# FFN input weights: the low half of each second 1024 columns comes from an accumulating DMA instead of a VectorE subtraction

## The chip, the core and the metric

The kernel runs on one core of a Trainium2 chip. The metric is the device time of one execution in microseconds (us). The profile is of one execution of the program, with the instructions of TensorE (PE, and PEld for its weight loads), VectorE (DVE), ScalarE (ACT), GpSimd (POOL) and the issuing queue of SyncE (SP), and with the packets of the core's 16 DMA engines.

## The reference, cut to what matters

One layer of a streaming encoder: two feed-forward networks (FFN) around a mixer and a cross attention. 256 tokens, 2048 features, FFN width 5504, all in float32.

```python
def swiglu_ffn(x, w_in, w_out):
    g, u = jnp.split(x @ w_in, 2, axis=-1)
    return (jax.nn.silu(g) * u) @ w_out
...
h = layer_norm(ALPHA * h + 0.5 * swiglu_ffn(h, ffn1_w_in[l], ffn1_w_out[l]), ln_ffn1_g[l], ln_ffn1_b[l])
mix = hybrid_mixer(h, ...)
h = layer_norm(ALPHA * h + mix, ln_mix_g[l], ln_mix_b[l])
xa = memory_cross_attention(h, ...)
h = layer_norm(ALPHA * h + xa, ln_x_g[l], ln_x_b[l])
h = layer_norm(ALPHA * h + 0.5 * swiglu_ffn(h, ffn2_w_in[l], ffn2_w_out[l]), ln_ffn2_g[l], ln_ffn2_b[l])
```

The change is in the products `x @ w_in` of both FFNs. `w_in` has 2 x 5504 columns: 43 tiles of 128 columns for the gate g and 43 for the other factor u.

## The kernel before, in words

**Exact halves.** TensorE multiplies float32 operands in a rounded form (`F32R`). To keep the precision, each operand is split into two halves: hi is the operand rounded to that form, lo is what is left (operand minus hi). A product is then three passes: hi by hi, hi by lo, lo by hi. Activations are split once; weights are split when they arrive.

**Weights.** The program is a list of items; each item names the weights that it needs, as pieces of [128, 2048] float32 (1 MB). `run` walks the list and, before it emits an item, emits the loads of the weights ahead (`load`, line 154). A load does this:

- line 157: one DMA on SP's queue brings the piece into a tile `raw`. There are 3 such tiles (`wraw`).
- for each of the two halves of 1024 columns ("first" and "second" below), line 162: a pair of tiles, `hi` and `lo` [128, 1024]. There are 4 of each (`UNITS = 4`, pools `whi` and `wlo`), so two pieces' worth.
- line 164: ScalarE casts the raw half to `hi`.
- line 167: VectorE subtracts, `lo = raw - hi`.

A pool gives a tile out again when its last reader is done, so the cast of line 164 waits until TensorE has finished with the piece two places earlier.

**The products.** `mm_wide` (lines 211 to 217) computes a tile of 128 output columns: for each of 16 K tiles one matmul with `hi` as weights and both halves of the activation as 512 moving columns (L216), and one with `lo` as weights and the high half as 256 columns (L217). The first 8 K tiles use the first half of the piece, the last 8 the second. `total` (lines 219 to 228) adds the two parts of the PSUM tile: a copy on ScalarE (L223, or L226 where it also scales) and an addition on VectorE (L224, or L227). `act` in `ffn` then takes silu on ScalarE (L420), the product on VectorE (L422) and splits the result (L195, L196).

**The stages.** The first FFN's input products fill two stretches of the program (24 and 19 pairs of tiles), each followed by the output products (L236). The first two pairs of the first FFN are loaded in quarters by `start` and not by `load`; the first four gate tiles of the second FFN are computed with tokens on partitions (`gates`), from another array, whose loads use blocks of their own or the same slots.

**GpSimd.** Its queue is almost empty before: the gains and biases of the layer norms (`gb_apply`, L324 and L325, eight DMAs in each of three places), the relative bias of the attention (L694), the memory tokens and their transpose (L867 `mem`, L869 `memT`) and the last gains (L1012).

**What sets the order.** The order on each engine is fixed when the program is built, by a scheduler that follows the order of the code with priorities; each engine executes its own list in order, and waits on semaphores of the others.

Of the kernel before, what the change touches and what calls it, by code (L numbers as in the profile page):

```python
# [13 lines left out]
ALU = mybir.AluOpType  # L14
AX = mybir.AxisListType
PSUM = bass.MemoryType.PSUM

P = 128
S = 256
D = 2048  # L20
# [20 lines left out]
# columns of the vector of per-partition parameters  # L41
# [13 lines left out]
class Act:  # L55
    """Activations, features on partitions, as exact halves: blocks of 4 tiles [P, 4, 2, S]."""
# [15 lines left out]
class Kernel:  # L72
# [50 lines left out]
    def add(self, fn, *weights, held=0, prio=0):  # L123
        """fn(units): a step with its weights, each an AP of up to 2048 columns, or (AP, tags) where the
        halves go into two blocks of their own, and a third tag, "early", lets them go there further
        ahead; held: unit slots of earlier items still in use."""
        self.items.append((fn, weights, held, prio))
# [4 lines left out]
    def collect(self, build, *args):  # L132
        """the items that build(*args) adds, as a list of their own."""
        kept, self.items = self.items, []
        build(*args)
        got, self.items = self.items, kept
        return got

    def weave(self, main, side, prio=SOON):
        """add main; side maps the number of main items done to steps to add then."""  # L140
        for i in range(len(main) + 1):
            for f in side.get(i, ()):
                self.add(f, prio=prio, held=main[i][2] if i < len(main) else 0)
            if i < len(main):
                self.items.append(main[i])

    def run(self):
        queue = [w if isinstance(w, tuple) else (w, None) for _, ws, _, _ in self.items for w in ws]
        ready, nxt, live = [], 0, 0

        def slots(w):
            return 0 if w[1] else -(-w[0].shape[1] // 1024)

        def load(ap, tags):
            n = ap.shape[1]
            raw = self.raw_tile()
            self.last_load = self.nc.sync.dma_start(raw[:, :n], ap)
            if tags:
                blk = [self.block(g, (P, 2048), F32R) for g in tags[:2]]
            got = []  # L160
            for c in range(0, n, 1024):
                m = min(1024, n - c)
                hi, lo = [x[:, c:c + 1024] for x in blk] if tags else self.unit()
                self.nc.scalar.copy(hi[:, :m], raw[:, c:c + m])  # L164
                # not between the short dependent steps of a layer norm's statistics
                with self.tc.issue_after(self.chain.ins) if self.chain is not None else nullcontext():
                    self.nc.vector.tensor_tensor(lo[:, :m], raw[:, c:c + m], hi[:, :m].bitcast(F32), ALU.subtract)  # L167
                got.append((hi, lo))
            return got

        def early(w):
            return w[1] is not None and len(w[1]) > 2

        def ahead(need, held):
            if nxt < need:
                return True
            n = sum(not early(w) for w in queue[need:nxt])
            return (nxt < need + 5 and (early(queue[nxt]) or n < 2)
                    and held + live + slots(queue[nxt]) <= UNITS)

        done = 0
        for fn, ws, held, prio in self.items:
            need = done + len(ws)
            while nxt < len(queue) and ahead(need, held):
                live += slots(queue[nxt])
                ready.append(load(*queue[nxt]))
                nxt += 1
            units = [u for _ in ws for u in ready.pop(0)]
            live -= sum(slots(queue[done + i]) for i in range(len(ws)))
            done = need  # L190
            with self.prio(prio):
                fn(units) if ws else fn()
# [6 lines left out]
    def mm_feat(self, ps, w, cols, x, kts):  # L199
        """ps [128 features, S]; cols[j] = (unit, column) of the j-th K tile."""  # L200
        n = len(kts)
        for j, kt in enumerate(kts):
            u, c = cols[j]
            for k, (wi, xi) in enumerate(PASSES):
                self.nc.tensor.matmul(  # L205
                    ps, w[u][wi][:, c:c + P], x.at(xi, kt),
                    start=(j == 0 and k == 0), stop=(j == n - 1 and k == 2),
                )

    def mm_wide(self, ps, w, x, n=KT):  # L210
        """the same over n K tiles of a 128-column tile: the products with the low half of x go to
        ps[:, S:], for `total` to add."""
# [6 lines left out]
    def total(self, ps, out=None, scale=1.0):  # L219
        """scale * (ps[:, :S] + ps[:, S:])"""  # L220
# [9 lines left out]
    def mm_tok(self, ps, tt, w, x, kts, start, stop):  # L230
        """ps [128 tokens of tile tt, 512 features]; two K tiles a unit."""
# [10 lines left out]
    def rsqrt(self, v, y, a):  # L242
        """y <- 1/sqrt(v); v is overwritten by -v/2."""
# [29 lines left out]
    def ln_T(self, h, mr, tt, ln, xT, qs=range(4)):  # L273
        """normalise h in place (without gain and bias) and write (n*g + b)^T, split, into xT."""
        nc = self.nc
        mean, r, nb = mr
        for q in qs:
# [6 lines left out]
            # not before the products that cover the statistics  # L284
# [16 lines left out]
    def ln_steps(self, ln, st, x):  # L301
        """what follows a finished residual tile: three groups of steps up to its part of x["T"]."""
# [15 lines left out]
    def gb_apply(self, i, h):  # L318
        """h <- h * g + b for both token tiles, g and b along the features."""
# [27 lines left out]
    def mask_out(self, b):  # L347
        """the first chunk of a query tile does not see the second chunk of its own key tile."""
        for c in (64, 320):
            self.nc.gpsimd.memset(b[0:64, c:c + 64], NEG)  # L350

    def start(self):
        """x^T and the first four weight tiles arrive in quarters of K, and are used as they come."""
# [50 lines left out]
    def ffn(self, tag, xT, st, first=None, steps=None, late=None, before=None, tags=None):  # L404
        """first: the PSUM tiles of the first two pairs of gate and up; before: what is left of the layer
        norm of token tile 1, to go between the first gates of token tile 0."""
# [45 lines left out]
    def gates(self, xT, before):  # L452
        """silu of the first 512 gate columns with tokens on partitions, token tile 0 first, then turned."""
# [35 lines left out]
    def out_proj(self, wname, k0, nk, x, scale, st, steps=None, tags=None):  # L489
        """h <- h (times ALPHA where scale) + x @ w[K tiles k0..]; with st, the statistics of the result.  # L490
        With `steps`, the last columns are done for token tile 0 first, and steps(0), what follows
        that tile, while they are done for tile 1."""
# [46 lines left out]
    def skewed(self, part, steps, tags=None):  # L539
        """four weight chunks, in unit slots or in blocks of their own, for token tile 0, then for 1."""  # L540
# [36 lines left out]
    def mixer(self, xT, st, steps):  # L577
# [4 lines left out]
        # values of A: tokens on partitions; the first columns for token tile 0 first  # L582
# [31 lines left out]
        # latents: features on partitions, RMS norm through a product with ones  # L614
# [35 lines left out]
        def swap(dst, src):  # L650
            """exchange the halves of each rotary vector (32 partitions each)."""
# [13 lines left out]
        # A: pairs of heads; products of the next pair cover the softmax of this one  # L665
# [13 lines left out]
        def scores(parts, spans_q):  # L679
            """parts: (q [K, S], k [K, S]) summed; returns the PSUM tile."""  # L680
# [31 lines left out]
        def pv(ps, v, pT):  # L712
            """ps [features, S] = sum over keys of v[key tile] and pT, causal tiles only."""
# [14 lines left out]
        # B: rotary parts of the queries of all heads  # L728
# [98 lines left out]
        # gates, output projections of A and B, and their mix  # L827
# [30 lines left out]
    def mem_norm(self):  # L858
        """steps: the statistics from the tokens, then the norm of the transposed memory in K-quarters."""
# [11 lines left out]
        def stat():  # L871
            """the diagonals of the means and of 1/deviation."""
# [10 lines left out]
        def spread():  # L883
            """both along the tokens, on every partition."""
# [167 lines left out]
def _feat(w):  # L1052
    """[K, N] -> [N/128, 128, K]: one tile of 128 columns, its K tiles side by side."""
# [4 lines left out]
def _tok(w):  # L1058
    """[K, N] -> [N/512, 128, K/128 * 512]."""
# [8 lines left out]
def _layout(i):  # L1068
# [35 lines left out]
    # the relative bias of each (query, key): query tile 0 with key tile 0, query tile 1 with both  # L1104
# [28 lines left out]
```

## Time and profile before

| | |
|---|---|
| time, two runs | 2585.01 and 2586.49 us, median 2585.75 |
| span of the profiled execution, first to last instruction | 2583.1 us |
| PE busy | 2565.8 us (99%) |
| DVE busy | 1568.2 us (61%) |
| ACT busy | 1229.6 us (48%) |
| POOL busy | 29.8 us (1%) |
| granted TensorE clock, mean | 0.998 |
| DMA | 488.20 MB, mean 189 GB/s |
| L167, VectorE's subtraction of weights, 128x1024 | 844 times, 1.22 us each |

How to read it: busy times are sums over an engine's instructions; TensorE's matmuls are pipelined, so its busy time says that it had work in flight, not how fast it went. A row of the timeline gives the start, the duration, the engine, the line, the operation with its output and input, and in square brackets how long the engine was idle before it and what released it. In rows of groups the mean is in nanoseconds. A row of DMA issues gives the tile and its source, the issuing queue, the count, the size of each and the median time from issue to landing in us. A row of a stretch (A:B, in us from the start of the span) gives its length, then the busy time and in parentheses the instructions of PE, PEld, DVE, ACT and POOL, then granted clock, mean busy share of the 16 DMA engines, and GB/s. A row of DMA queues gives the packets, the MB and the share of the 16 engines' time; q1 is SP's queue, q0 GpSimd's.

### The profile page before, as it was taken

How to read it: one execution, taken by the hardware profiler on the slowest of the kernel's cores; microseconds unless marked ns; L12 is line 12 of the kernel's file. 1: busy time of each engine (PE TensorE's matmuls, PEld its weight loads, DVE VectorE, ACT ScalarE, POOL GpSimd, SP SyncE). 2: the span in 40 equal slices, each digit the busy share in tenths (PEclk: the TensorE clock that was granted, in tenths of full speed). 3: DMA queues.
4: the chain of work that ended last, by engine and by line, in shares of the span. 5: the costliest groups of instructions: out<-in, count | busy, mean ns of one | idle time of the engine just before them, and what ended most of it. 6: DMA issues, size and time to landing. Idle time of an engine off the chain costs nothing.

```text
span 2583.1 us, 34485 instructions
## 1 busy us (share of the span) xinstructions
PE 2565.8 (99%) x13844; PEld 2195.0 (85%) x13844; DVE 1568.2 (61%) x2208; ACT 1229.6 (48%) x1809; POOL 29.8 (1%) x87
## 2 busy tenths in 40 slices
PE   9999999999999999999999999999999999999998
PEld 8888888888888888888888888888888888888886
DVE  6555545555675776655657784555865554455556
ACT  5444434444454555544444554454644443344432
POOL 0000000000000000000000000000000000000000
PEclk9999999999999999999999999999999999999999
DMA  7655555555655643355556565544555555555563
GB/s 256 223 194 188 189 194 195 180 191 180 235 183 184 195 150 104 141 186 188 194 189 256 192 212 190 193 163 142 196 202 194 191 185 194 196 184 191 181 220 137
DMA packets 74448, 488.20 MB, mean 189 GB/s; under 512 B 8496, under 2 KB 8752, under 8 KB 20016
## 3 DMA queue, kind: packets, MB, share of 16 engines
q1 hardware_dynamic: 69360, 468.17, 51.7%
q0 software_dynamic: 3808, 15.73, 1.9%
q8 instruction: 108, 1.77, 0.3%
q10 hardware_dynamic: 1120, 2.10, 0.2%
q14 instruction: 52, 0.43, 0.1%
HBM read 482.69 MB, written 2.10 MB: 188 GB/s over the span
## 4 chain that ended last, share of the span: by engine, by line
PE 99%; DVE 0%; DMA 0%; ACT 0%; issue 0%; DVEq 0%; ACTq 0%
PE mm L216 40%; PE mm L236 32%; PE mm L217 20%; PE mm L205 2%; PE at L684 1%; PE at L567 1%; PE at L714 1%; PE mm L384 1%; PE at L984 0%; PE at L962 0%; PE at L288 0%; DMA raw<-ffn_w_in 0%; PE mm L385 0%; PE at L715 0%; PE at L634 0%; DVE h L1021 0%
## 5 line engine op out<-in xcount | busy, mean ns | idle before, releaser
L167 DVE TENSOR_TENSOR lo<-raw,hi 128x1024 fp32r<-128x1024 f32 x850 | 1035.4, 1220 | 893.1 <-ACT hi L164 880.2
L164 ACT CAST hi<-raw 128x1024 fp32r<-128x1024 f32 x850 | 887.8, 1046 | 1005.3 <-PE mm L216 384.3
L216 PE MATMUL mm<-T,hi 128*128 128x512 f32 x3792 | 1330.0, 396 | 0.0
L217 PE MATMUL mm<-T,lo 128*128 128x256 f32 x3792 | 1057.8, 279 | 0.0
L216 PEld LDWEIGHTS mm<-T,hi 128*128 128x128 f32 x3792 | 711.7, 188 | 171.8 <-issue 1.5
L217 PEld LDWEIGHTS mm<-T,lo 128*128 128x128 f32 x3792 | 714.0, 188 | 0.2
L236 PE MATMUL mm<-hi,H 128*128 128x512 f32 x1640 | 506.9, 389 | 0.0
L236 PEld LDWEIGHTS mm<-hi,H 128*128 128x128 f32 x1640 | 307.8, 188 | 63.8
L236 PE MATMUL mm<-lo,H 128*128 128x512 f32 x820 | 319.1, 389 | 0.0
L216 PE MATMUL mm<-H,hi 128*128 128x512 f32 x640 | 223.3, 394 | 0.0
L236 PEld LDWEIGHTS mm<-lo,H 128*128 128x128 f32 x820 | 153.9, 188 | 31.9
L217 PE MATMUL mm<-H,lo 128*128 128x256 f32 x640 | 177.5, 277 | 0.0
L216 PEld LDWEIGHTS mm<-H,hi 128*128 128x128 f32 x640 | 120.0, 188 | 27.7
L236 PE MATMUL mm<-hi,X 128*128 128x512 f32 x416 | 130.4, 391 | 0.0
L217 PEld LDWEIGHTS mm<-H,lo 128*128 128x128 f32 x640 | 120.2, 188 | 0.0
L236 PEld LDWEIGHTS mm<-hi,X 128*128 128x128 f32 x416 | 77.9, 188 | 16.1 <-issue 0.2
L224 DVE TENSOR_TENSOR w<-w,mm 128x256 f32<-128x256 f32 x195 | 80.8, 414 | 12.6 <-ACT w L223 12.5
L420 ACT ACTIVATE w<-w 128x256 f32<-128x256 f32 x82 | 34.3, 419 | 109.0 <-DVE w L224 109.0
L236 PE MATMUL mm<-lo,X 128*128 128x512 f32 x208 | 81.0, 389 | 0.0
L223 ACT COPY w<-mm 128x256 f32<-128x256 f32 x203 | 74.0, 364 | 0.5 <-PE mm L385 0.5
L195 ACT CAST H<-w 128x256 fp32r<-128x256 f32 x110 | 44.3, 402 | 34.6 <-DVE w L224 27.3
L205 PE MATMUL mm<-X,hi 128*128 128x256 f32 x320 | 59.6, 286 | 0.0
(172 smaller groups left out, 1521.2 us busy)
## 6 DMA issues: line engine op xcount, KB each, us to landing
raw<-ffn_w_in SPq DMA_DIRECT2D x167, 1024.0 KB, 4.8
raw<-ffn_w_out SPq DMA_DIRECT2D x80, 1024.0 KB, 4.8
raw<-w_gate SPq DMA_DIRECT2D x36, 1024.0 KB, 4.8
raw<-w_qk SPq DMA_DIRECT2D x16, 1024.0 KB, 4.9
raw<-w_o_b SPq DMA_DIRECT2D x16, 1024.0 KB, 4.8
raw<-w_out SPq DMA_DIRECT2D x16, 1024.0 KB, 4.9
raw<-w_xk SPq DMA_DIRECT2D x16, 1024.0 KB, 4.8
raw<-w_xv SPq DMA_DIRECT2D x16, 1024.0 KB, 4.8
```

The costliest lines, as they stand in the source:

```text
L164: self.nc.scalar.copy(hi[:, :m], raw[:, c:c + m])
L167: self.nc.vector.tensor_tensor(lo[:, :m], raw[:, c:c + m], hi[:, :m].bitcast(F32), ALU.subtract)
L195: self.nc.scalar.copy(hi, src)
L205: self.nc.tensor.matmul(ps, w[u][wi][:, c:c + P], x.at(xi, kt), start=(j == 0 and k == 0), stop=(j == n - 1 and k == 2),)
L216: self.nc.tensor.matmul(ps, hi, x.both(kt), start=(kt == 0), stop=False)
L217: self.last_mm = self.nc.tensor.matmul(ps[:, :S], lo, x.at(0, kt), start=False, stop=(kt == n - 1))
L223: self.nc.scalar.copy(t, ps[:, S:])
L224: self.nc.vector.tensor_tensor(t if out is None else out, t, ps[:, :S], ALU.add)
L236: self.last_mm = self.nc.tensor.matmul(ps, x.at(xi, kt)[:, tt * P:(tt + 1) * P], w[u][wi][:, c:c + 512], start=(start and j == 0 and k == ...
L384: nc.tensor.matmul(ps[c], w[0], xT.both(kt), start=(kt == 0), stop=False)
L420: nc.scalar.activation(s, s, AF.Silu)
L567: self.nc.tensor.transpose(ps[:, i * P:(i + 1) * P], s[:, c:c + P], self.ident)
```

## The change

For each piece of `ffn1_w_in` and `ffn2_w_in` that goes through the unit slots, the second half's `lo` is made differently: ScalarE writes the negated raw half into `lo`, which as a tile of the rounded form holds -hi, and a DMA issued by GpSimd adds the raw half onto it. The source of that DMA is the weight in HBM for the first FFN and the raw tile in SBUF for the second. First halves, and all other weights, keep the subtraction on VectorE.

```diff
     def run(self):
         queue = [w if isinstance(w, tuple) else (w, None) for _, ws, _, _ in self.items for w in ws]
         ready, nxt, live = [], 0, 0
+        route = {}
+        for i, (ap, tags) in enumerate(queue):
+            if ap.tensor.name in ("ffn1_w_in", "ffn2_w_in") and tags is None:
+                route[i] = "hbm" if ap.tensor.name == "ffn1_w_in" else "sbuf"
...
-        def load(ap, tags):
+        def load(ap, tags, how=None):
...
                 self.nc.scalar.copy(hi[:, :m], raw[:, c:c + m])
+                if c and how is not None:
+
+                    self.nc.scalar.mul(lo[:, :m], raw[:, c:c + m], -1.0)
+                    src = ap[:, c:c + m] if how == "hbm" else raw[:, c:c + m]
+                    self.nc.gpsimd.dma_start(lo[:, :m], src, accum_op=ALU.add)
+                    got.append((hi, lo))
+                    continue
+
                 with self.tc.issue_after(self.chain.ins) if self.chain is not None else nullcontext():
                     self.nc.vector.tensor_tensor(lo[:, :m], raw[:, c:c + m], hi[:, :m].bitcast(F32), ALU.subtract)
...
-                ready.append(load(*queue[nxt]))
+                ready.append(load(*queue[nxt], how=route.get(nxt)))
```

The lines after it move down by 4 to 11: the cast of line 164 is line 168 in the new kernel, the negation is line 171, the DMA 173, the subtraction 178, and `total`'s copies 234 and 237. The other lines of the diff take comments out.

In ScalarE's list, the steady state of the first FFN, before (`hi`, `lo` and `raw` are the tiles above, `w` and `H` are the SwiGLU's intermediate and the hidden activation, `mm` a PSUM tile; a number is a tile's own):

```order
L164 CAST hi_591<-raw_589 128x1024
L195 CAST H_43_338<-w_75_540 128x256
L164 CAST hi_595<-raw_589 128x1024
L223 COPY w_88_632<-mm_556 128x256
L420 ACTIVATE w_88_632<-w_88_632 128x256
L164 CAST hi_644<-raw_642 128x1024
L164 CAST hi_648<-raw_642 128x1024
L226 ACTIVATE w_89_636<-mm_599 128x256
```

The same place in the list of the changed kernel:

```order
L168 CAST hi_597<-raw_595 128x1024
L168 CAST hi_601<-raw_595 128x1024
L171 ACTIVATE lo_602<-raw_595 128x1024
L234 COPY w_88_639<-mm_562 128x256
L431 ACTIVATE w_88_639<-w_88_639 128x256
L168 CAST hi_651<-raw_649 128x1024
L168 CAST hi_655<-raw_649 128x1024
L237 ACTIVATE w_89_643<-mm_606 128x256
L171 ACTIVATE lo_656<-raw_649 128x1024
L206 CAST H_44_341<-w_89_643 128x256
```

The negation stands right behind the cast of the second half in one piece of a pair, and behind the scaled copy (L237) in the other; the cast of the hidden activation (L195, now L206) has moved from between the two casts of a piece to ahead of them. TensorE's list is the same row by row but for the numbers; VectorE's has 1972 rows in place of 2136.

In GpSimd's list, around the start of the second FFN, before (`w` are the layer norm's gains and biases):

```order
L324 DMA w_2303_14187<-gb 128x512
L325 DMA w_2304_14188<-gb 128x512
L324 DMA w_2621_16223<-gb 128x512
L325 DMA w_2622_16224<-gb 128x512
L324 DMA w_2623_16231<-gb 128x512
L325 DMA w_2624_16232<-gb 128x512
```

In the changed kernel (the first and the last of the eight gain and bias loads stand for all of them, with "..." between):

```order
L335 DMA w_2303_14269<-gb 128x512
L336 DMA w_2304_14270<-gb 128x512
L173 DMA lo_16186<-raw_16179 128x1024
L173 DMA lo_16209<-raw_16202 128x1024
L335 DMA w_2621_16308<-gb 128x512
...
L336 DMA w_2628_16333<-gb 128x512
L173 DMA lo_16304<-raw_16297 128x1024
L173 DMA lo_16386<-raw_16379 128x1024
L173 DMA lo_16436<-raw_16429 128x1024
```

Two accumulating DMAs of the second FFN stand ahead of the eight gain and bias loads, the other 80 behind them. The 82 of the first FFN stand in one run ahead of the first gain loads of the program.

## The prediction

> **What bounds the kernel now.** I read the page's first and fourth parts first, then the busy time by stretches of the two feed-forward stages, then ScalarE's timeline inside one of them, and last the DMA views.
>
> ```profile
> span 2583.1 us, 34485 instructions
> PE 2565.8 (99%) x13844; PEld 2195.0 (85%) x13844; DVE 1568.2 (61%) x2208; ACT 1229.6 (48%) x1809; POOL 29.8 (1%) x87
> PE 99%; DVE 0%; DMA 0%; ACT 0%; issue 0%; DVEq 0%; ACTq 0%
> ...
> 1885.00:2120.00 235.00, 235.00 (x1358) 205.51 (x1357) 140.69 (x184) 113.77 (x170) 0.00 (x0) 1.00 0.56 192
> ```
>
> TensorE is busy 99% of the span and is 99% of the chain that ended last. In the stretch 1885 to 2120 us, which holds the first part of the second feed-forward layer's input products, it is busy 235.00 of 235.00 us at a granted clock of 1.00 (the columns after the stretch are its length, then PE, PEld, DVE, ACT, POOL, then clock, DMA share, GB/s). What is idle on it in the whole span is 2583.1 - 2565.8 = 17.3 us, 0.7%. VectorE, which the change relieves, stands on no part of that chain. So nothing is there to gain beyond 0.7%; the question is only whether TensorE starts to wait. 2% (52 us) is about what a measurement of this kernel can tell from no change.
>
> **The slack of a weight half.** The hi casts of ScalarE in the steady state show the rhythm:
>
> ```profile
> 153.20 1.05 ACT L164 CAST hi<-raw 128x1024 fp32r<-128x1024 f32 x1 [1.52 <-PE mm L216]
> 154.15 0.38 ACT L226 ACTIVATE w<-mm 128x256 f32<-128x256 f32 x1
> 155.96 1.05 ACT L164 CAST hi<-raw 128x1024 fp32r<-128x1024 f32 x1 [1.43 <-issue]
> ...
> 158.75 1.05 ACT L164 CAST hi<-raw 128x1024 fp32r<-128x1024 f32 x1 [1.43 <-PE mm L216]
> 159.70 0.37 ACT L223 COPY w<-mm 128x256 f32<-128x256 f32 x1
> ...
> 164.29 1.05 ACT L164 CAST hi<-raw 128x1024 fp32r<-128x1024 f32 x1 [1.52 <-PE mm L216]
> ```
>
> The casts at 153.20, 158.75 and 164.29 are those of second halves. Each starts when TensorE gives its slot back (the releaser in brackets). From 153.20 to 164.29 two weight tiles pass: 11.09 / 2 = 5.545 us a tile, 2.77 us a half. There are four slots, two tiles' worth. The slot of a second half comes free when TensorE ends a tile; TensorE then works a whole other tile (5.545) and the first half of the next (2.77), and wants the slot filled again after 8.32 us. Before, the filling takes a cast and a subtraction:
>
> ```profile
> 154.28 1.22 DVE L167 TENSOR_TENSOR lo<-raw,hi 128x1024 fp32r<-128x1024 f32 x1 [1.34 <-ACT hi L164]
> ```
>
> It ends at 155.50, 2.30 us after the slot came free; 6.0 us are to spare. The change spends from these 6.0 us.
>
> **The change part by part.** *Removed:* the order of VectorE falls from 2136 rows to 1972, 164 subtractions: 82 tiles in each feed-forward layer (86 less the four that the start or the gates handle). At 1.22 us that is 200 us of VectorE, worth nothing to the time, since TensorE covers it.
>
> *Added on ScalarE:* 164 negations of 128x1024. No such row exists; the cast of the same shape is the nearest:
>
> ```profile
> L164 ACT CAST hi<-raw 128x1024 fp32r<-128x1024 f32 x844 | 884.1, 1049 | 1003.5 <-PE mm L216 384.3 <-PE mm L236 373.6 <-issue 211.4
> ```
>
> 164 x 1.05 = 172 us, beside 1003.5 us that it idles before casts; about 1.05 more per 5.545 us where it is busy for some 2.9. It has the room, so the cost is delay alone: in one kind of tile the negation follows the cast directly (cast at 158.75, its follower starts at 159.70, so the negation would end at 160.75, 2.0 us after the release); in the other L226's 0.38 us lies between (follower starts at 154.15, then 0.33, then 1.05: 155.53, 2.33 after). I take 2.2 us. Were a negation as slow as VectorE's 1.22 us for this shape, the delay would grow by 0.17 us and the sum below by 0.17 / 2 x 164 = 14 us; I see no reason for it to be faster than the cast.
>
> *Added on POOL:* 164 DMA issues, each waiting for its negation. Issues on that queue:
>
> ```profile
> 1883.85 0.54 POOL L324 DMA_DIRECT2D w<-gb  x1
> 1884.38 0.54 POOL L325 DMA_DIRECT2D w<-gb  x1
> ```
>
> 0.54 us a piece, one per 5.545 us: the queue itself is no bound. The order puts all 82 of the first layer ahead of the first gain loads (L324/L325), so there nothing waits behind anything else. In the second layer the third accumulating DMA stands behind eight gain loads; the last of them was issued at 1884.38 + 0.54 = 1884.92, and the subtraction that it replaces began at 1883.99:
>
> ```profile
> 1883.99 1.22 DVE L167 TENSOR_TENSOR lo<-raw,hi 128x1024 fp32r<-128x1024 f32 x1
> ```
>
> So that queueing costs under 1 us, once, inside the 6 us of slack.
>
> *Added on the DMA engines:* this is the term that decides. Call L the time from issue to landing. TensorE waits when 2.2 + L exceeds 8.32, so from **L = 6.1 us** on. A slot serves every second tile, so an excess is spread over two tiles: the tile takes (2.2 + L + 2.77) / 2, the stall per tile is **(L - 6.1) / 2**, and 2% of the time (52 us over 164 tiles, 0.32 each) is reached at L = 6.75. No accumulating DMA is in the trace. The nearest rows:
>
> ```profile
> raw<-ffn_w_in SPq DMA_DIRECT2D x167, 1024.0 KB, 4.8
> ...
> raw<-w_o_a SPq DMA_DIRECT2D x16, 512.0 KB, 3.4
> ...
> DMA to landing us min/median/max: 5.1/6.2/7.3
> DMA to landing us min/median/max: 9.4/11.2/13.0
> ```
>
> The last two are the memory tokens (two loads of 1024 KB from POOL, back to back) and their transpose (two more right behind). A plain 512 KB lands in 3.4 us. An accumulation must fetch the 512 KB that is added and the 512 KB it is added to, so it is nearer to a 1024 KB transfer: 5.1 us at best on that queue. The lower end is 3.4 (the second fetch costs nothing), the upper 13.0 (it behaves like a transfer behind three others).
>
> [...]
>
> It isn't alone either: a 1024 KB weight load is due in each tile's time. How the engines share is shown where the memory loads ran beside weight loads, 1368 to 1390 us:
>
> ```profile
> 1374.00:1380.00 6.00, 6.00 (x36) 5.25 (x35) 6.00 (x10) 2.78 (x4) 1.05 (x2) 1.00 0.98 401
> ...
> q0 software_dynamic: 576, 4.19, 48.1%
> q1 hardware_dynamic: 582, 4.18, 47.1%
> ...
> raw<-w_out SPq DMA_DIRECT2D x4, 1024.0 KB, 8.8
> ```
>
> At a DMA share of 0.98, 48.1% of 22 us carried 4.19 MB: 2.5 us of all 16 engines per MB, so 2.6 us for 1024 KB. Per tile: 2.6 for the load, 2.6 for the accumulation with two fetches, 5.2 of 5.545 us. It fits, at 94% use, but there is no room to land quickly. In the first layer the load's raw tile comes free with the same negation that releases the accumulation, so both start together and share: about 2.1 us that don't scale with size (3.4 less half of the 2.6 us) and 2 x 2.6 us of data, **L = 7.3 us**; the slower of the two overlapping 1024 KB loads above took 7.3 as well. In the second layer the raw tile comes free only when the accumulation has read it, and the next load starts into the next accumulation; I take the same L. Stall: (7.3 - 6.1) / 2 = 0.6 us a tile, 164 x 0.6 = **98 us**.
>
> *The sum:* own execution 2583.1 us span, -0 for VectorE, -0 for TensorE's order (its rows are the same), +98: 2681 us of span; the median of the runs shown, 2585.75, lies 2.65 above the span, so 2684 us.
>
> **The rivals.** *Hidden* (not slower): the second fetch overlaps the first, or load and accumulation fall into different parts of the 5.545 us. For it: the DMA engines are only 0.56 busy in the stretch above, and 1024 KB from POOL landed in 5.1 us once beside weight loads. Against: the load is freed by the instruction that frees the accumulation. It holds up to L = 6.1 and counts as no change up to 6.75: 2586 us. [...]
>
> *Heavier*: adding row by row keeps the engines longer than two fetches, and the queue backs up as for the transposed memory. At 9.4 us: 1.65 x 164 = 271 us, 2857 us; at 11.2: 418 us, 3004 us; at 13.0: 566 us, 3152 us. For it: nothing of the kind was ever run in this kernel, and at 94% use a little more work is a lot more wait. Against: 401 GB/s was moved with a full TensorE.
>
> *The ring of three raw tiles* becomes the bound in the second layer. It goes around in load (8.8 us where the DMA was full) + cast, cast and negation (some 3.3) + accumulation (7.3) = 19.4 us for three tiles, 6.45 a tile: 0.9 x 82 = 74 us there, and 0.6 x 82 = 49 us in the first layer: 2709 us. Against: with a load of 4.8 us it is 15.4 us, under 3 x 5.545 = 16.6.
>
> *The change isn't what it says*: excluded by the order, which holds 164 negations and 164 DMAs.
>
> **How the numbers follow.** Slower by 2 to 8% (two fetches, shared; the ring belongs here): 0.40. Hidden: 0.34. Heavier, over 8%: 0.24. Faster by over 2% has only 17.3 us to draw on: 0.02 for what I don't see. So faster 0.02, same 0.34, slower 0.64. The likeliest gives 2684 us, its own range is L from 6.75 to 8.5: 2639 to 2783 us. The range as a whole takes in the hidden case and the lower end of the heavier one: 2583 to 2880 us.
>
> **What will show it.** Right: landing of the accumulations near 7.3 us, TensorE idle before L217 or its weight load with a DMA onto lo as releaser, a tile time near 6.1 us in both layers, DMA share near 0.9. Wrong on the low side: landing under 6.1 and TensorE still at 235 of 235; on the high side: landing over 8.5 us, or POOL or the DMA share full. If one layer alone slows, the source (HBM or the raw tile) matters and I treated them as one.

## The result, and the profile after

The changed kernel took 2766.2 us (2763.16 to 2769.24, two runs) against 2585.75 us: slower by 180 us, ratio 1.0683, 95% interval 1.066 to 1.0706. The forecast was 2684 us with a range of 2583 to 2880 us, and slower by over 2% at 0.64.

First the page of the changed kernel: span, busy times, the DMA queues (packets, MB, share of the 16 engines' span), the chain that ended last.

```profile
span 2761.3 us, 34962 instructions
PE 2616.7 (95%) x13844; PEld 2211.9 (80%) x13844; DVE 1389.0 (50%) x2044; ACT 1393.8 (50%) x1973; POOL 171.8 (6%) x251
q1 hardware_dynamic: 69360, 468.17, 48.9%
q0 software_dynamic: 27424, 101.73, 18.4%
PE 62%; DMA 23%; issue 11%; ACT 3%; DVE 0%; POOL 0%; SPq 0%; POOLq 0%; ACTq 0%; DVEq 0%
```

VectorE lost 179 us of work and ScalarE gained 164 (200 and 172 were costed). The chain is no longer TensorE's alone: 23% of it is now transfers. Where they stand in it shows in the chain of waits between 153 and 167 us, in the first FFN (start, duration, what; L227 and L228 are the old L216 and L217):

```profile
156.53 0.04 ACT hi L168
156.57 0.91 issue
157.48 1.05 ACT lo L171
158.53 0.27 ACT w L234
158.80 0.03 issue
158.83 8.58 DMA lo<-ffn_w_in
167.40 0.04 issue
167.45 0.39 PE mm L228
```

This is the round of a slot: TensorE gives it back at 156.53, cast and negation end at 158.53, the DMA is issued at 158.83, lands 8.58 us later at 167.40, and 0.04 us after that TensorE starts the half that waited for it. TensorE's rows with idle time show the same from its side, in both layers:

```profile
153.70 0.39 PE L228 MATMUL mm<-T,lo 128*128 128x256 f32 x1 [1.56 <-DMA lo<-ffn_w_in]
160.18 0.38 PE L228 MATMUL mm<-T,lo 128*128 128x256 f32 x1 [0.56 <-DMA lo<-ffn_w_in]
167.45 0.39 PE L228 MATMUL mm<-T,lo 128*128 128x256 f32 x1 [1.35 <-DMA lo<-ffn_w_in]
```

```profile
2205.14 0.39 PE L228 MATMUL mm<-T,lo 128*128 128x256 f32 x1 [1.74 <-DMA lo<-raw]
2217.73 0.39 PE L228 MATMUL mm<-T,lo 128*128 128x256 f32 x1 [1.02 <-DMA lo<-raw]
2230.46 0.39 PE L228 MATMUL mm<-T,lo 128*128 128x256 f32 x1 [1.17 <-DMA lo<-raw]
```

TensorE's waits for the accumulations in the whole execution, taken at its weight loads (total, times, longest), in the first and in the second FFN:

```profile
PEld mm L228 <- DMA lo<-ffn_w_in: 103.2, 75, 4.3
PEld mm L228 <- DMA lo<-raw: 59.6, 38, 3.7
```

In the first FFN nearly every tile stalls (75 of 82; 13.75 us from 153.70 to 167.45 for two tiles, 6.9 a tile); in the second about every other one (38 of 82; 12.6 to 12.7 us for two, 6.3 a tile). The page's issues with their median landings, and from the view of the accumulations' line the landings (min/median/max) in the first and in the second FFN:

```profile
raw<-ffn_w_in SPq DMA_DIRECT2D x167, 1024.0 KB, 5.9
lo<-ffn_w_in POOLq DMA_DIRECT2D x82, 512.0 KB, 8.0
lo<-raw POOLq DMA_DIRECT2D x82, 512.0 KB, 6.1
```

```profile
DMA to landing us min/median/max: 7.7/8.0/11.1
DMA to landing us min/median/max: 4.5/6.1/9.5
```

What else moves at that time differs between the layers. In the first FFN a weight load starts with each accumulation (the load at 158.56 us, the accumulation at 158.83). In the second it starts when an accumulation has landed (the load at 2111.22, the landing at 2111.09) and runs into the next one (issued at 2111.81).

How much each part lost is read from SP's load issues (count, duration in ns, first to last start): the first load of the mixer's values (`w_va`) ends the first FFN, the last of the cross attention's output weights (`w_xo`) begins the second. Before, then after:

```profile
L157 SPq DMA_DIRECT2D raw<-w_xo x16: 327/328/328, 1721.4 to 1821.3; - x16
...
L157 SPq DMA_DIRECT2D raw<-w_va x8: 327/328/328, 699.7 to 744.1; - x8
```

```profile
L161 SPq DMA_DIRECT2D raw<-w_xo x16: 327/328/328, 1837.0 to 1936.9; - x16
...
L161 SPq DMA_DIRECT2D raw<-w_va x8: 327/328/328, 809.6 to 854.1; - x8
```

The first FFN lost 110 us (699.7 to 809.6). The stages between lost another 6 us (1936.9 - 809.6 against 1821.3 - 699.7), without an edit there; the kernel below that adds on VectorE loses the same 6 us there, and the one with HBM in both layers none, so they hardly belong to the accumulations. The second FFN lost 63 us (what is left of 2761.3 - 2583.1).

### The profile page after: what moved, and what is told of

It reads as the page before. It is cut to its first block, busy times and chain, and to the rows that moved or that the text cites. A ratio compares the mean times of both kernels' runs of the same rounds, so it can differ in the third digit from the quotient of the medians.

```text
span 2761.3 us, 34962 instructions
## 1 busy us (share of the span) xinstructions
PE 2616.7 (95%) x13844; PEld 2211.9 (80%) x13844; DVE 1389.0 (50%) x2044; ACT 1393.8 (50%) x1973; POOL 171.8 (6%) x251
## 3 DMA queue, kind: packets, MB, share of 16 engines
q0 software_dynamic: 27424, 101.73, 18.4%
## 4 chain that ended last, share of the span: by engine, by line
PE 62%; DMA 23%; issue 11%; ACT 3%; DVE 0%; POOL 0%; SPq 0%; POOLq 0%; ACTq 0%; DVEq 0%
PE mm L247 25%; PE mm L227 21%; DMA lo<-ffn_w_in 13%; PE mm L228 11%; DMA lo<-raw 9%; PE mm L216 2%; ACT lo L171 2%; PE at L695 1%; DMA raw<-ffn_w_in 1%; PE at L725 1%; PE at L578 1%; ACT hi L168 0%; PE at L995 0%; PE at L973 0%; ACT w L234 0%
## 5 line engine op out<-in xcount | busy, mean ns | idle before, releaser
L227 PE MATMUL mm<-T,hi 128*128 128x512 f32 x3792 | 1352.8, 399 | 0.0
L178 DVE TENSOR_TENSOR lo<-raw,hi 128x1024 fp32r<-128x1024 f32 x686 | 834.6, 1219 | 735.5 <-ACT hi L168 718.2
L228 PE MATMUL mm<-T,lo 128*128 128x256 f32 x3792 | 1082.3, 285 | 127.4 <-DMA lo<-ffn_w_in 79.3
L227 PEld LDWEIGHTS mm<-T,hi 128*128 128x128 f32 x3792 | 718.5, 189 | 168.8 <-issue 1.5
L228 PEld LDWEIGHTS mm<-T,lo 128*128 128x128 f32 x3792 | 722.7, 191 | 163.1 <-DMA lo<-ffn_w_in 103.2
L227 PE MATMUL mm<-H,hi 128*128 128x512 f32 x640 | 225.9, 397 | 0.0
L228 PE MATMUL mm<-H,lo 128*128 128x256 f32 x640 | 178.9, 279 | 0.0
L171 ACT ACTIVATE lo<-raw 128x1024 fp32r<-128x1024 f32 x164 | 172.6, 1053 | 0.3
L227 PEld LDWEIGHTS mm<-H,hi 128*128 128x128 f32 x640 | 120.2, 188 | 29.1
L173 POOL DMA_DIRECT2D lo<-raw x82 | 70.8, 864 | 909.4 <-ACT lo L171 638.5
L228 PEld LDWEIGHTS mm<-H,lo 128*128 128x128 f32 x640 | 120.6, 189 | 0.0
L238 DVE SCALAR_TENSOR_TENSOR w<-mm,w 128x256 f32<-128x256 f32 x86 | 36.5, 424 | 161.0 <-ACT w L237 161.0
L173 POOL DMA_DIRECT2D lo<-ffn_w_in x82 | 71.1, 867 | 647.8 <-ACT lo L171 359.1
```

What stands on the lines that cost most here:

```text
L171: self.nc.scalar.mul(lo[:, :m], raw[:, c:c + m], -1.0)
L173: self.nc.gpsimd.dma_start(lo[:, :m], src, accum_op=ALU.add)
L227: self.nc.tensor.matmul(ps, hi, x.both(kt), start=(kt == 0), stop=False)
L228: self.last_mm = self.nc.tensor.matmul(ps[:, :S], lo, x.at(0, kt), start=False, stop=(kt == n - 1))
L238: self.nc.vector.scalar_tensor_tensor(t if out is None else out, ps[:, :S], scale, t, ALU.mult, ALU.add)
```

## The experiments

Ten kernels ran. Each is given against runs of the kernel before on the same chip, whose medians were 2590.8, 2591.0 and 2590.8 us in the three sets.

**Source in SBUF in both layers; source in HBM in both.**

```diff
-                route[i] = "hbm" if ap.tensor.name == "ffn1_w_in" else "sbuf"
+                route[i] = "sbuf"        # and "hbm" in the second kernel
```

> The source of the accumulation is the raw tile in SBUF in both layers. Between before and the change the first FFN lost 110 us (the first load of the mixer's values moved from 699.7 to 809.6 us) and the second 68 us. Theory A (the source decides: with the source in HBM the weight load is free to start with the accumulation and both share the DMA engines): the first FFN loses as the second does, 2586 + 2 x 68 = 2722 us, landing near 6.1 us in both layers. Rival B (the first layer is dearer for its place in the program): no difference, 2766 us.

> The source is HBM in both layers. Theory A: 2586 + 2 x 110 = 2806 us, landing near 8.0 us in both layers. Rival B: 2766 us.

Measured: 2753.2 us (ratio 1.0611, 1.057 to 1.0651) from SBUF, 2792.4 us (1.0769, 1.0749 to 1.0789) from HBM. With HBM in both, the landings are 8.0 us in both, `w_va`'s first load comes at 806.2 us, and the profiled executions lost 107 us in the first FFN and 105 in the second: the layers are alike, so the place in the program isn't what made the first dearer (rival B falls), and the time is 14 us under theory A's. With SBUF in both, landings fall to 5.9 and 5.5 us and the losses to 92 and 79 us, but the time only to 2753, some 30 us more than theory A had. The source decides, but for less than I had put down to it. Part of what was missing turned up in the granted clock; it is shown in the last section.

**A plain copy in place of the accumulation.**

```diff
-                    self.nc.gpsimd.dma_start(lo[:, :m], src, accum_op=ALU.add)
+                    self.nc.gpsimd.dma_start(lo[:, :m], src)
```

> The DMA copies the raw half over the negated one without adding, so lo holds the weights themselves and not the remainder; everything else stays, the negation too. Theory A (the landing is long because the accumulation fetches its destination as well: 2.8 us of all 16 engines each by the changed kernel's queue row, 18.4% of 2761 us less 49 us of the other transfers, over 164): about half that time of the engines, landing near 5 us, under the 6.1 us that the slot allows, TensorE doesn't wait: 2586 to 2610 us. Rival C (the cost is in the software queue, its issue of 0.87 us and its 128 rows): landing stays at 6 to 8 us and the time near 2766 us.

Measured: 2641.6 us (1.0191, 1.0172 to 1.021), 51 us over before, where the accumulation cost 180 on the other chip. From the page of the copying kernel, with a span of 2631.9 us, the queue and the landings for both sources:

```profile
q0 software_dynamic: 27424, 101.73, 11.0%
...
lo<-ffn_w_in POOLq DMA_DIRECT2D x82, 512.0 KB, 5.8
lo<-raw POOLq DMA_DIRECT2D x82, 512.0 KB, 4.7
```

The same packets and bytes are counted, but 11.0% of 2631.9 us less the 49 us of the other transfers (1.9% of 2583.1 us before), over 164, is 1.47 us of all engines for a copy, against (18.4% of 2761.3 - 49) / 164 = 2.80 us for an accumulation: 1.9 times. That is about what a second fetch of the same size would take; the bytes that the queue counts don't show the fetch itself. Rival C falls. Theory A was too hopeful by 30 us: 5.8 us at the median stands right at the edge of the slack, and the later ones stall.

**The negation ahead of the cast.**

```diff
-                self.nc.scalar.copy(hi[:, :m], raw[:, c:c + m])
                 if c and how is not None:
-                    self.nc.scalar.mul(lo[:, :m], raw[:, c:c + m], -1.0)
+                    neg = self.nc.scalar.mul(lo[:, :m], raw[:, c:c + m], -1.0)
...
                     self.nc.gpsimd.dma_start(lo[:, :m], src, accum_op=ALU.add)
+                    with self.tc.issue_after(neg.ins):
+                        self.nc.scalar.copy(hi[:, :m], raw[:, c:c + m])
                     got.append((hi, lo))
                     continue
+                self.nc.scalar.copy(hi[:, :m], raw[:, c:c + m])
```

> ScalarE negates the second half before it casts it, so the accumulation is issued about 1.0 us earlier after the slot came free (1.3 us where the scaled copy lay between). Theory A (a chain of latencies: slot free, negation, issue, landing, half a tile of TensorE): half of that per tile, 0.5 to 0.65 us x 164 = 80 to 105 us less where every tile stalls, 2660 to 2690 us. Rival D (the throughput of the DMA engines is the bound, at a share of 0.91 in the first FFN): what is won is waited for in the queue, landing grows by 1 us, the time stays within 2750 to 2766 us.

Measured: 2718.2 us (1.0483, 1.0459 to 1.0507), 127 us over before, 53 less than the change's 180: between the two. The first FFN gave back 41.5 us (`w_va` at 768.1 in place of 809.6), 0.5 a tile as theory A had it. There the accumulations land no later (8.1 us at the median, 8.0 in the change), although the weight loads do (7.7 us between 100 and 200 us, 5.7 in the change). The second gave back nothing. There the long landings grew, as rival D had it for all: 15 of the 82 take over 9 us, where the change has 2. The granted clock was 0.98 there (2020 to 2230 us), where the change has 0.99 (1990 to 2225 us; the last section has its price).

**The weight loads of the first FFN left out.** All its routed pieces read one raw tile, loaded once.

```diff
+        fixed = []
...
-            raw = self.raw_tile()
-            self.last_load = self.nc.sync.dma_start(raw[:, :n], ap)
+            if how == "hbm":
+                if not fixed:
+                    fixed.append(self.block("X0", (P, 2048)))
+                    self.last_load = self.nc.sync.dma_start(fixed[0], ap)
+                raw = fixed[0]
+            else:
+                raw = self.raw_tile()
+                self.last_load = self.nc.sync.dma_start(raw[:, :n], ap)
```

> In the first FFN the 82 pieces are all read from one raw tile that is loaded once, so 81 loads of 1024 KB are left out (the products are of the wrong weights); the accumulations from HBM stay as they are. Theory A (an accumulation alone takes about 2.1 us plus 2.8 us of engine time, and the rest of its 8.0 us is the weight load that starts with it): landing near 5 us, under the 5.9 us that the slot allows, TensorE doesn't wait in the first FFN, which gives back its 110 us: 2766 - 110 = 2656 us. Rival E (an accumulating DMA is that slow by itself): landing stays near 8 us, 2766 us.

Measured: 2677.8 us (1.0336, 1.0305 to 1.0367). TensorE's waits in this kernel (total, times, longest) and the landings in its first FFN:

```profile
PE mm L235 <- DMA lo<-raw: 48.1, 31, 3.1
PE mm L235 <- DMA lo<-ffn_w_in: 5.1, 5, 3.3
```

```profile
DMA to landing us min/median/max: 5.2/5.4/9.7
```

Without the weight loads, the accumulation from HBM lands in 5.4 us and the first FFN hardly waits: it lost 10 us (`w_va` at 709.6). So 2.6 of its 8.0 us are the weight loads beside it, as the prediction had it; rival E falls. The time stays 22 us over theory A's, as these 10 us are left and the second FFN, where nothing was edited, lost 71 us here and 63 in the change.

**The addition on VectorE, the negation kept.**

```diff
-                    src = ap[:, c:c + m] if how == "hbm" else raw[:, c:c + m]
-                    self.nc.gpsimd.dma_start(lo[:, :m], src, accum_op=ALU.add)
+                    with self.tc.issue_after(self.chain.ins) if self.chain is not None else nullcontext():
+                        self.nc.vector.tensor_tensor(lo[:, :m], raw[:, c:c + m], lo[:, :m].bitcast(F32), ALU.add)
```

> ScalarE's 164 negations stay, but VectorE adds the raw half onto them and no DMA does. Theory A (172 us more on ScalarE lie under TensorE, only the transfer's time from issue to landing costs): as before, 2586 us, within 10. Rival F (ScalarE's order, later casts and sums, holds TensorE up): a part of the 180 us stays, more than 20.

Measured: 2595.4 us, ratio 1.0014 (0.9998 to 1.0029): no difference within 0.3%, with ScalarE at 1392.9 us of work. The negations cost nothing that can be measured; rival F falls.

**Every second piece only.**

```diff
-        route = {}
+        route, seen = {}, 0
...
             if ap.tensor.name in ("ffn1_w_in", "ffn2_w_in") and tags is None:
+                seen += 1
+                if seen % 2:
+                    continue
                 route[i] = "hbm" if ap.tensor.name == "ffn1_w_in" else "sbuf"
```

> Only every second piece gets its second low half from the accumulating DMA (41 in each FFN), the others from VectorE as before; the DMA bytes that the change adds are halved, to about 4.4 us of engine time per 5.545 us. Pieces take the slots in turn, so the accumulated ones always meet in the same slots, and one round of such a slot is two tiles, 11.09 us. Theory A (the round of the slot: 2.3 to the issue, landing, 2.77): where the landing stays at 7.5 to 8 us, as the weight load still starts with it, the first FFN loses 1.5 to 2.0 us per accumulated piece, 60 to 82 us, the second 0 to 25: 2646 to 2693 us. Half of the DMA work would then save well under half of nothing but the second FFN's loss. Rival D (throughput of the DMA engines): 80% use leaves room, 2586 to 2605 us.

Measured: 2689.4 us (1.0399, 1.0372 to 1.0426), 99 us over before. TensorE's waits on the accumulations (total, times, longest; in the second FFN they come to 0.8 us), two stretches, of the first and the second FFN's input products, and the page's issues:

```profile
PEld mm L231 <- DMA lo<-ffn_w_in: 86.2, 41, 4.2
```

```profile
100.00:200.00 100.00, 86.02 (x462) 72.92 (x461) 38.39 (x51) 46.18 (x65) 6.04 (x7) 0.97 0.67 197
2070.00:2170.00 100.00, 100.00 (x568) 86.67 (x567) 46.31 (x62) 57.46 (x81) 7.74 (x9) 1.00 0.73 230
```

```profile
lo<-ffn_w_in POOLq DMA_DIRECT2D x41, 512.0 KB, 7.9
lo<-raw POOLq DMA_DIRECT2D x41, 512.0 KB, 4.5
```

This is the sharpest of them. In the first FFN half of the accumulations cost nearly as much as all of them, 102 us (`w_va` at 801.3) against 110: the 41 pieces stall all 41 times, with the DMA engines at 0.67 only. That is more than theory A's 60 to 82 us; its total came out because the second FFN lost only 2. The landing is still 7.9 us, as the load still starts with it (at 107.14 us the load, at 107.40 the accumulation), and the round of the slot is the same two tiles. In the second FFN, where the load isn't released by the negation, the landing is 4.5 us and TensorE is busy 100 of 100 us. The share of 0.67 was no room here: started beside a load, no accumulation of the first FFN landed in under 7.6 us.

**Six lo tiles.** Two more lo tiles are paid for with one raw tile; the negation and its DMA come first, with the source in HBM; a second kernel has the same for every second piece; a third is the kernel before with these buffers.

```diff
-        self.wraw = pool("wraw", 3)
+        self.wraw = pool("wraw", 2)
-        self.wlo = pool("wlo", UNITS)
+        self.wlo = pool("wlo", UNITS + 2)
...
+            if how is not None:
+                u = [self.unit() for _ in range(2)]
+                neg = self.nc.scalar.mul(u[1][1], raw[:, 1024:2048], -1.0)
+                self.nc.gpsimd.dma_start(u[1][1], ap[:, 1024:2048], accum_op=ALU.add)
+                with self.tc.issue_after(neg.ins):
+                    self.nc.scalar.copy(u[0][0], raw[:, :1024])
...
```

> Six lo tiles in place of four (paid for by two raw tiles in place of three), the negation of a piece ahead of its casts, and the source in HBM in both FFNs. A lo slot comes free one tile earlier, so the accumulation has some 11 us to land, where it had 5.9. The same bytes are moved. Theory A (latency against the slack of the slots): no stall is left but at the start, 2590 to 2620 us. Rival D (the DMA engines' throughput: 3.0 us for a load and 2.8 us for an accumulation against 5.545 us a tile): the tile goes no lower than 5.8 us and more when queues form, 2630 us or over, with the DMA share at 1.0.

> The kernel before with two raw tiles in place of three and six lo tiles in place of four: what these buffers alone do to the time. Every theory: 2586 us, up to 15 more if the loads come late somewhere. It is what the run with six lo tiles is to be read against.

> Every second piece as in the run before, with the source in HBM, six lo tiles, two raw tiles and the negation first in those pieces: both the slack and the throughput are there. If latency against slack and, behind it, the throughput are all that the change costs, it runs as the kernel before does with these buffers (2597 us): 2592 to 2605 us. If more than 10 us over that are left, a third cost is missing from the account.

Measured: 2636.9 us (1.0186, 1.0156 to 1.0216) with all pieces, 2597.3 us (1.0019, 1.0001 to 1.0037) for the buffers alone, 2610.3 us (1.0077, 1.0053 to 1.0101) with every second piece. The kernel with all pieces: a stretch in its first FFN, the page's issues, and ScalarE's negations with what they waited for:

```profile
100.00:200.00 100.00, 97.27 (x552) 84.17 (x551) 34.73 (x50) 60.14 (x85) 14.58 (x17) 1.00 1.00 274
```

```profile
raw<-ffn_w_in SPq DMA_DIRECT2D x167, 1024.0 KB, 7.6
lo<-ffn_w_in POOLq DMA_DIRECT2D x164, 512.0 KB, 7.7
```

```profile
L167 ACT ACTIVATE lo<-raw 128x1024 fp32r<-128x1024 f32 x164 | 173.9, 1061 | 332.7 <-DMA raw<-ffn_w_in 330.4
```

Landings near 8 us, which cost 202 us with HBM in both layers, cost 40 us when the slot has one more tile of time and the negation goes first (which alone gave back 41.5 us in one such layer). What stays fits the throughput: the DMA share is 1.00, and 40 / 164 = 0.24 us a tile makes 5.79 us, what rival D had for this kernel (5.8). But the ring of the two raw tiles gives nearly the same. The negations now wait for the weight loads, 330.4 us in all, and hardly for TensorE. A load issued at 105.83 us lands at 113.04, its piece is negated, cast and subtracted by 116.70, and the next load into that tile starts at 116.76; this round and the two behind it take 10.8 to 11.6 us, 5.4 to 5.8 us a tile. So the slack of the slot is one limit, and behind it stand the full DMA engines, or the ring of two raw tiles whose loads take 7.6 us there and 4.8 in the control. No run separates these two: six lo tiles with three raw tiles were not tried. With every second piece 13 us over the control are left, 3 more than I allowed for. Of those, 5.5 us are TensorE's waits for accumulations (two, the longer of 4.4); the rest I can't place.

## Why the prediction was right, and what it mis-sized

*No gain from VectorE, no cost on ScalarE:* right, the second shown (to 0.3%) by the kernel that negates on ScalarE and adds on VectorE.

*The step that decides, landing time against the slack of the slot, with (landing - threshold) / 2 for a tile:* right. The prediction put the threshold at 6.1 us. In the trace GpSimd issues 0.30 us after the negation ends (158.53 to 158.83), where VectorE had started 0.03 us after ScalarE; with the 0.3 us it is about 5.9.

*Two fetches, and a weight load released by the same instruction:* that an accumulation moves like 1024 KB was my estimate, and no run counts a second fetch; in the engines' time it fits (1.47 us for the plain copy against 2.80). The second is borne out by the kernel without the loads (5.4 against 8.0 us) and by the start times (0.27 us apart).

*The sum, 98 us, was too small by nearly half; the term that failed in size is the landing.* I took 7.3 us for both layers. In the first the median was 8.0 us and the mean of the 82 landings in the trace 8.4: (8.38 - 5.9) / 2 x 82 = 102 us, where I had 49. Measured were 110 us. In the second the median was 6.1 us and the mean 6.2, which by the formula cost 8 to 14 us; measured were 63. There I mis-read the shape and not only the size: short and long landings mostly alternate (4.5 to 9.5 us), and halving the excess is right only where both slots are late. Where one is late and the other not, the tile waits for the late one and the early one gives nothing back.

This can be worked out from the trace, landing by landing, as an estimate: a tile ends 5.545 us after the tile before it, or 2.44 + L + 2.88 us after the tile two places before, whichever is later. Here 2.44 is the mean of the 2.30 and 2.57 us from the slot's return to the issue, and 2.88 the time from a landing to the end of the tile (167.40 to 170.28). With the landings of the changed kernel this gives 106 us in the first FFN and 61 in the second, against 110 and 63 measured. So the mechanism accounts for both layers, and only little is left for the granted clock. That my 49 us for the second layer came near its 63 is luck: its median landing alone would have meant next to no stall. I treated the two sources as one, and said what that would look like if wrong; the runs with one source in both layers and with every second piece showed that it was.

*The rivals.* Hidden: no. Heavier: no, an accumulation takes the engines no longer than two copies (2.80 against 2 x 1.47 us) and lands in 5.4 us without the weight loads, in 8.0 beside one. The ring of three raw tiles wasn't shown as a bound by any run; with two raw tiles and six lo tiles it may be one.

*The checks it named:* landing near 7.3 us (8.0 and 6.1), TensorE released by a DMA onto lo (yes), tiles near 6.1 us (6.9 and 6.3), DMA share near 0.9: 0.90 in the first (20 to 320 us, below) and 0.89 in the second (1990 to 2225 us).

## What to carry to other kernels

The work that left VectorE for a DMA here left a step of 1.22 us for one of 4.5 (every second piece, second FFN) to 8.0 (the change, first FFN): set the landing against the slack of the buffer, round by round, before counting what the engine saves. Take the landing as it is beside the transfers that the same instruction releases (8.0 us here), not that of the transfer alone (5.4); the average DMA share doesn't show that (0.67 here, with every accumulation of the first FFN late). An accumulation kept the DMA engines busy 1.9 times as long as a copy of the same size (2.80 against 1.47 us). A buffer more, with the negation first, turned most of the loss away (202 us to 40) until the DMA share was 1.00.

## What the runs showed of the hardware that I had not expected

A short stall of TensorE cost more here than its own length. Windows of the changed kernel around one:

```profile
49.00:52.30 3.30, 1.40 (x9) 0.98 (x8) 1.65 (x2) 1.45 (x3) 0.86 (x1) 1.00 0.70 190
52.40:55.70 3.30, 3.30 (x12) 2.81 (x11) 0.00 (x0) 0.00 (x0) 0.00 (x0) 0.50 0.94 238
55.80:59.00 3.20, 3.20 (x19) 2.64 (x17) 0.42 (x1) 2.45 (x4) 0.64 (x1) 1.00 0.28 58
```

After 3.3 us in which TensorE was busy for 1.40, the next 3.3 us were granted half the clock (column before the last two), though it was busy all through: 12 matmuls in place of 19. Before its last instructions the changed kernel's clock fell so nine times, each time for 3.41 us; in the 3.41 us ahead TensorE had been busy for 0.34 to 1.53 us. Behind the 3.41 us from 2045.74, in which it was busy for 1.50, the clock stayed at 1.00, so the time it was busy ahead doesn't settle alone where the clock falls. Its price at most, from the granted clock over long stretches; first the changed kernel, then the one with both sources in SBUF:

```profile
20.00:320.00 300.00, 257.33 (x1363) 215.47 (x1361) 91.25 (x134) 157.90 (x217) 36.02 (x42) 0.97 0.90 232
320.00:815.00 495.00, 457.90 (x2277) 381.02 (x2277) 200.34 (x232) 239.02 (x293) 35.09 (x41) 1.00 0.77 219
...
1937.00:2560.00 623.00, 583.70 (x3046) 494.01 (x3045) 257.56 (x355) 337.25 (x439) 64.81 (x78) 0.99 0.79 232
```

```profile
20.00:320.00 300.00, 268.14 (x1443) 229.82 (x1443) 95.49 (x139) 165.60 (x227) 38.02 (x44) 0.95 0.86 243
320.00:795.00 475.00, 445.15 (x2185) 374.75 (x2184) 193.75 (x223) 230.75 (x282) 32.74 (x38) 0.97 0.74 220
...
1920.00:2560.00 640.00, 595.66 (x3047) 504.56 (x3046) 258.23 (x356) 336.97 (x440) 64.69 (x78) 0.97 0.77 226
```

0.03 x 300 + 0.01 x 623 is 15 us of clock in the change; 0.05 x 300 + 0.03 x 475 + 0.03 x 640 is 48 us with both sources in SBUF. Those 33 us are about what that kernel ran over its expectation. Its mean granted clock is 0.982, where the change has 0.993, and its stalls are fewer and longer (64 waits of 2.1 us, where the change has 113 of 1.4). That longer stalls make the clock fall more often is my reading; no run set them apart. An accumulating DMA also kept GpSimd busy for 0.86 us per issue (the change), a plain one for 0.53 (the plain copy).
